# Channel mixer of a decoder block: partial products summed in PSUM banks, three token operands stored already split, gates applied to results

## The chip, the cores and the metric

The kernel runs on one core of a Trainium2 chip, as one program. The metric is the time of the whole program on the device, in microseconds (us); lower is better. A profile of one execution shows what each engine did: TensorE (PE, with PEld for its weight loads), VectorE (DVE), ScalarE (ACT), GpSimd (POOL) and SyncE (SP), whose queue issues most of the DMAs.

## The reference

The block takes 1024 tokens of 1024 features. It normalizes them, mixes tokens in two head groups, adds the result to the scaled input and normalizes again. The change lies in what follows, the channel mixer and the last norm:

```python
x = layer_norm(ALPHA * x + gt1 * mix, ln1_g, ln1_b)
h = x * (1.0 + sc2) + sh2
gu = h @ w_ffn_in                                     # 1024 x 1024 by 1024 x 5632
f = (silu(gu[..., :2816]) * gu[..., 2816:]) @ w_ffn_out   # 1024 x 2816 by 2816 x 1024
x = layer_norm(ALPHA * x + gt2 * f, ln2_g, ln2_b)
```

All of it is float32. The gates `gt1` and `gt2` are vectors over the 1024 output features.

## The kernel before

**Precision.** A float32 operand of a matmul is held as two parts: `hi`, the operand rounded (an ACT copy to the rounded type), and `lo`, the rest (a DVE subtraction). A product is three matmuls, hi x hi, hi x lo and lo x hi. Making the two parts is called a split here: one ACT and one DVE instruction on 128 x 512 elements, in `comb` (L1241 to L1247) for the first product and in `split2` (L1458 to L1463) for the second.

**Seven products for eight.** Each of the two large products is cut in halves of tokens, rows and columns and done in Winograd's form of Strassen's scheme, so that seven products of halves take the place of eight. The price is sums: of operands ahead of the products and of results behind them.

**First product** (`Col`, L1254 to L1313, and the loop at L1431). The 2816 hidden columns are 22 tiles of 128. For each the kernel loads 512 KB of gate weights and 512 KB of value weights. Seven times `prod` splits a 128 x 512 weight operand and runs 12 matmuls into one PSUM bank. Products `p1` and `p2` use the first half of the tokens (`a1h`, `a1l`), the other five (p5, p6, p7, p3, p4) use five sums of token halves (`a2h`, `a2l`: S3, S4, A22, S1, S2, made between L1413 and L1427). Each product has a PSUM bank of its own. The seven results are summed by DVE out of PSUM into SBUF tiles (`s1`, `u4`, `c22`; L1286, L1293, L1310). The sums of weights (`tsum`, L1396) are on POOL, and so are the two products with the silu (L1307, L1312). Two column tiles, kk and kk + 11, make a pair: from their results `f0`, `f1` POOL forms the sums (L1430, L1451) that become the seven token operands of the second product, QA11 to QS4, and SP's queue stores these in DRAM (`put`, L1442). The first three tiles' `p1` and `p2` are done earlier, among the transposes of the last token tiles.

**Second product** (`product`, L1504 to L1555). Seven calls, in the order QA11, QS1, QS2, QA22, QS3, QA12, QS4. Each goes through 11 steps of 128 rows. In a step the token operand `fs` and the weight operand `ws` are split into a ring of six tiles, and 12 matmuls run: three for each of four token tiles, each of which has a PSUM bank. `fs` comes from DRAM, two steps in one load. The weights are four blocks of 11 x 128 x 512: B11, B12, B21, B22. B11 is rewritten in place between the calls (T1 = B12 - B11, T2 = B22 - T1, T4 = T2 - B21) by DVE, B12 once by POOL (L1623, L1636, L1637, L1665), a step at a time in the functions `pre5`, `pre6`, `pre4`. Two operands, B21 and B22, take the gate `gt2` in their columns on POOL (L1666, L1695). The functions `done2` to `done7` (and `copied`) make generators that take results out of PSUM; `product` runs them a stage at a time between the steps of the next product (`pending`). They add gated results to the rows `R[t]`, which hold eight token tiles. `skip2` (L1493) has put the scaled and shifted first norm there, on POOL and DVE, during the second product. Each call takes four fresh banks. In the last call (`tail=5`) the matmuls of the last five steps are ordered by token tile, so that the banks finish one after the other. `norm2` (L1563) is the last norm of a token tile. In it POOL raises the variance to the power -1/2, ACT scales, POOL (and DVE for one half of tiles 0 to 2) applies gain and bias, and SP's queue stores. Tiles 4 to 7 get it during QA12, tiles 0 to 3 after QS4.

The order of instructions on each engine is decided when the program is compiled: the framework orders them by program order and its estimate of readiness, and inserts all semaphores. Instructions that go through `add` (L1560) keep their program order on their engine. On the chip each engine runs its list in order.

Of the kernel before, what the change touches and what calls it, by code (L numbers as in the profile page):

```python
# [9 lines left out]
F32 = mybir.dt.float32  # L10
# [61 lines left out]
SD0 = 8  # L72
GELU_A = math.sqrt(2.0 / math.pi)
# [4 lines left out]
def kernel(ctx, tc, inp, out, dbg=None):  # L78
# [12 lines left out]
    # ------------------------------------------------------------------ pools  # L91
# [26 lines left out]
    # -------------------------------------------------------------- constants  # L118
# [21 lines left out]
    # ------------------------------------- small vectors, one per partition  # L140
# [21 lines left out]
    for i, (n, ap) in enumerate(vecs):  # L162
# [9 lines left out]
        # the 32 gate columns stand three times side by side  # L172
# [13 lines left out]
    # derived columns: 1-mu (15), 0.5*w0, 0.5*a0, -, 0.5*k_a, 1-0.5*k_a, 0.5*sgg  # L186
# [7 lines left out]
    # --------------------------------------------------------- layer norm bits  # L194
# [11 lines left out]
    # ---------------------------------------------------------------- weights  # L206
# [40 lines left out]
    def ada(b, pool):  # L247
        """Half b of the columns of shift and scale: modc = silu(c) @ w_ada + b_ada."""
# [24 lines left out]
    with sctx:  # L273
# [8 lines left out]
        def hrs(hf):  # L282
            """Half hf of the tokens, normalized and feature-major."""
# [17 lines left out]
        for k in range(NK):  # L301
# [3 lines left out]
            # the small vectors come between the large ones  # L305
# [70 lines left out]
        with masks:  # L376
            # -------------------------------------------------------------- masks
# [43 lines left out]
            # chunk parity e keeps its removal-key scores, scaled by TS, on partitions 64 e  # L421
# [15 lines left out]
        # ------------------------------------- low-rank inputs of the decay, rate and gate  # L437
# [26 lines left out]
        # hi and lo parts; the 32 last rows carry hi, lo, hi against hi, hi, lo  # L464
# [23 lines left out]
        # ------------------------------------- spatial weights, transposed and masked  # L488
# [10 lines left out]
        # cgd[d, g, t] = 0.5 * (b[d] * sum_s W[t, s] + b_s[t])  # L499
# [14 lines left out]
    # ============================================ RWKV-7 and gMLP, feature-major  # L514
# [3 lines left out]
    # block diagonal over the two chunks of a tile  # L518
# [20 lines left out]
    def rwkv(q, hf, zr, zk, zv, carry):  # L539
# [37 lines left out]
        # ---- in-context rate (2a - 1)  # L577
# [6 lines left out]
        # ---- normalised removal key  # L584
# [17 lines left out]
        # ---- key, bonus  # L602
# [29 lines left out]
        # ---- scores: partition = (key, source token), free = (tile, parity, head, [A|R] target token)  # L632
# [36 lines left out]
        # ---- Z = (I - T)^-1 by doubling the size of the inverted diagonal blocks; Y = Z^T  # L669
# [24 lines left out]
        # T is held as 1024 T = T1 + T2 in halves of its width; the level masks carry 1 / 1024.  # L694
# [41 lines left out]
        # two correction terms bring the half-width inverse to full width:  # L736
        # E = I - Z (I - T), inverse = Z + E Z + E E Z
# [32 lines left out]
        # ---- U0 and A, solved  # L770
# [22 lines left out]
        # ---- chunk transition, its input, and the read-out rows  # L793
# [3 lines left out]
        # (tile, parity) = chunk; a parity has its own bank  # L797
# [32 lines left out]
        # ---- states  # L830
# [20 lines left out]
        # ---- read-out  # L851
# [10 lines left out]
        # ---- group norm, bonus, gate  # L862
# [24 lines left out]
    # ------------------------------------------------------------------ gMLP  # L887
# [16 lines left out]
    def late(c0, tail, side=iter(())):  # L904
        """The projections of four column tiles; the tail of each runs some steps into the next."""
# [66 lines left out]
    def modrest():  # L972
        # products and sums over the blocks of rows on the vector engine, the last sum on the tensor engine
# [58 lines left out]
    def mixout(t, wide=None):  # L1032
        """Token tile t of the output projection: two PSUM banks. The last rows of y come last."""
# [51 lines left out]
    def skip(t, x, ag, ab, second):  # L1085
        """alpha times the entry norm of token tile t."""
# [7 lines left out]
    def norm1(pool, t, x, sk, mo):  # L1094
        """x = the first norm of the skip and the output projection, without gain and bias."""
# [645 lines left out]
```

## Time and profile before

| | |
|---|---|
| Median of 3 runs | 1504.8 us (1504.12 to 1509.2) |
| Span of the profiled execution, first to last instruction | 1497.9 us |
| PE busy | 1356.2 us (91%) |
| DVE busy | 1062.1 us (71%) |
| POOL busy | 693.4 us (46%) |
| ACT busy | 509.2 us (34%) |
| Mean granted TensorE clock | 0.969 |
| First product's last part, second product's first matmul | up to 1206 us, 1206.3 us |
| Second product's last matmul ends | 1485.5 us |

The profiled execution's own time on the device was not recorded beside its span; the median of the runs lies 6.9 us above the span. Start times in the profile count from the start of the span. "Busy" is the time in which an engine had an instruction running, and matmuls overlap, so a busy PE may still run below its peak. In a group's row the first number after the bar is its busy time in us, then the mean in ns of one, and after the second bar the idle time ahead of it and what ended that. In a row of a stretch the columns are busy time and (count) for PE, PEld, DVE, ACT and POOL, then the granted TensorE clock as a share of full, the share of DMA engines' time in use, and GB/s. In a row of waits the columns are the total in us, how many, and the longest.

### The profile page before, as it was taken

How to read it: one execution, taken by the hardware profiler on the slowest of the kernel's cores; microseconds unless marked ns; L12 is line 12 of the kernel's file. 1: busy time of each engine (PE TensorE's matmuls, PEld its weight loads, DVE VectorE, ACT ScalarE, POOL GpSimd, SP SyncE). 2: the span in 40 equal slices, each digit the busy share in tenths (PEclk: the TensorE clock that was granted, in tenths of full speed). 3: DMA queues.
4: the chain of work that ended last, by engine and by line, in shares of the span. 5: the costliest groups of instructions: out<-in, count | busy, mean ns of one | idle time of the engine just before them, and what ended most of it. 6: DMA issues, size and time to landing. Idle time of an engine off the chain costs nothing. (4 is left out here: it accounts for less than half of the span.)

```text
span 1497.9 us, 23562 instructions
## 1 busy us (share of the span) xinstructions
PE 1356.2 (91%) x9279; PEld 1036.2 (69%) x9279; DVE 1062.1 (71%) x1615; ACT 509.2 (34%) x836; POOL 693.4 (46%) x596
## 2 busy tenths in 40 slices
PE   4879999999999998899879999999999997787986
PEld 3657666766766666667657888888888885565764
DVE  7734878786876887873899755555545458989997
ACT  4432323233232323331574333333333233332442
POOL 3672222121223244451457855555565327366584
PEclk9989999999999999999989999999999998898998
DMA  9423113222221222623403433323332278321222
GB/s 300 125 77 110 56 38 107 71 65 69 83 84 51 93 89 97 221 91 105 157 29 99 132 100 106 102 91 103 106 106 91 107 264 339 112 78 50 85 86 98
DMA packets 154057, 163.68 MB, mean 109 GB/s; under 512 B 9696, under 2 KB 111738, under 8 KB 153946
## 3 DMA queue, kind: packets, MB, share of 16 engines
q1 hardware_dynamic: 148810, 152.70, 31.4%
q10 hardware_dynamic: 4128, 6.32, 1.3%
q0 software_dynamic: 1008, 3.15, 0.6%
q8 instruction: 73, 1.20, 0.3%
q14 instruction: 38, 0.31, 0.1%
HBM read 124.65 MB, written 37.49 MB: 108 GB/s over the span
## 5 line engine op out<-in xcount | busy, mean ns | idle before, releaser
L1269 PE MATMUL p<-a2h,wc 128*128 128x512 f32 x440 | 173.7, 395 | 2.3 <-ACT wc L1245 2.3
L1271 PE MATMUL p<-a2h,wc 128*128 128x512 f32 x440 | 175.7, 400 | 0.0
L1270 PE MATMUL p<-a2l,wc 128*128 128x512 f32 x440 | 174.1, 396 | 0.0
L1513 PE MATMUL fo<-ws,fs 128*128 128x512 f32 x288 | 121.6, 422 | 39.7 <-DVE ws L1462 39.6
L229 PE MATMUL mm<-hh,wh 128*128 128x512 f32 x320 | 141.2, 441 | 2.8 <-ACT wh L216 2.8
L231 PE MATMUL mm<-hh,wl 128*128 128x512 f32 x320 | 132.0, 414 | 0.0
L230 PE MATMUL mm<-hl,wh 128*128 128x512 f32 x320 | 130.3, 407 | 0.0
L1512 PE MATMUL fo<-ws,fs 128*128 128x512 f32 x288 | 118.0, 413 | 4.6 <-ACT ws L1461 4.6
L1514 PE MATMUL fo<-ws,fs 128*128 128x512 f32 x288 | 118.6, 412 | 0.0
L1246 DVE TENSOR_TENSOR wc<-wr,wc 128x512 fp32r<-128x512 f32 x66 | 60.7, 921 | 74.9 <-ACT wc L1245 74.6
L1245 ACT ACTIVATE wc<-ts 128x512 fp32r<-128x512 f32 x88 | 55.1, 631 | 153.0 <-PE p L1271 136.5
L1513 PEld LDWEIGHTS fo<-ws,fs 128*128 128x128 f32 x288 | 57.5, 200 | 63.9 <-DVE ws L1462 52.5
L1269 PEld LDWEIGHTS p<-a2h,wc 128*128 128x128 f32 x440 | 82.9, 188 | 22.9 <-ACT wc L1245 3.3
L1270 PEld LDWEIGHTS p<-a2l,wc 128*128 128x128 f32 x440 | 83.0, 189 | 21.4 <-DVE a2l L1420 0.3
L1462 DVE TENSOR_TENSOR fs<-fr,fs 128x512 fp32r<-128x512 f32 x77 | 79.0, 1028 | 24.7 <-ACT fs L1461 24.6
L1271 PEld LDWEIGHTS p<-a2h,wc 128*128 128x128 f32 x440 | 82.9, 188 | 19.6 <-DVE wc L1246 0.3
L1462 DVE TENSOR_TENSOR ws<-b,ws 128x512 fp32r<-128x512 f32 x70 | 82.5, 1178 | 1.9 <-ACT ws L1461 1.6
L1398 POOL TENSOR_TENSOR ts<-ts,wr 128x512 f32<-128x512 f32 x22 | 30.3, 1377 | 106.1 <-DVE wc L1246 106.1
L1246 DVE TENSOR_TENSOR wc<-ts,wc 128x512 fp32r<-128x512 f32 x88 | 75.5, 862 | 2.9 <-ACT wc L1245 1.2
L1461 ACT ACTIVATE fs<-fr 128x512 fp32r<-128x512 f32 x77 | 47.9, 625 | 87.0 <-PE fo L1514 56.4
L229 PEld LDWEIGHTS mm<-hh,wh 128*128 128x128 f32 x320 | 60.9, 190 | 22.9 <-issue 6.7
L1269 PE MATMUL p<-a1h,wc 128*128 128x512 f32 x176 | 69.9, 397 | 3.9 <-ACT wc L1245 3.9
(518 smaller groups left out, 3379.5 us busy)
## 6 DMA issues: line engine op xcount, KB each, us to landing
wa<-in_w_ada_dram SPq DMA_DIRECT2D x48, 512.0 KB, 4.4
wr<-in_w_ffn_in_dram SPq DMA_DIRECT2D x44, 512.0 KB, 3.9
fr<-q SPq DMA_DIRECT2D x30, 512.0 KB, 3.8
wr<-in_w_in_dram SPq DMA_DIRECT2D x22, 512.0 KB, 4.3
q<-u SPq DMA_DIRECT2D x44, 256.0 KB, 3.2
q<-c SPq DMA_DIRECT2D x33, 256.0 KB, 2.2
b<-in_w_ffn_out_dram SPq DMA_DIRECT2D x6, 1024.0 KB, 13.0
x<-in_x_dram SPq DMA_DIRECT2D x8, 512.0 KB
```

The costliest lines, as they stand in the source:

```text
L229: T.matmul(ps[0:m, :], wh[:, k, 0:m], xh[:, k, cs], start=(k == 0), stop=False)
L230: T.matmul(ps[0:m, :], wh[:, k, 0:m], xl[:, k, cs], start=False, stop=False)
L231: T.matmul(ps[0:m, :], wl[:, k, 0:m], xh[:, k, cs], start=False, stop=(k == NK - 1))
L1245: A.activation(v[0], src, AF.Copy)
L1246: V.tensor_tensor(out=v[1], in0=src, in1=f(v[0]), op=ALU.subtract)
L1269: T.matmul(ps, w[:, 0, ks], h[:, o + k, :], start=k == 0, stop=False)
L1270: T.matmul(ps, w[:, 0, ks], l[:, o + k, :], start=False, stop=False)
L1271: T.matmul(ps, w[:, 1, ks], h[:, o + k, :], start=False, stop=k == 3)
L1462: V.tensor_tensor(out=t[:, 1, :], in0=src, in1=f(t[:, 0, :]), op=ALU.subtract)
L1512: T.matmul(pss[t], fs[:, 0, ts], ws[:, 0, :], start=kk == 0, stop=False)
L1513: T.matmul(pss[t], fs[:, 0, ts], ws[:, 1, :], start=False, stop=False)
L1514: T.matmul(pss[t], fs[:, 1, ts], ws[:, 0, :], start=False, stop=kk == NH - 1)
```

## The change

It edits the two products of the channel mixer and the last norm. Lines of comment that it also drops are not shown.

1. First product: the seven products of a column tile use three banks in place of seven. `p1` and the former `p2` share one, products of t2, t1 and u1 share `b`, two others share `e`. DVE reads a bank between the additions to it (two reads of `b` and one of `e` before the last one), and ACT reads `p1`'s. DVE has 5 sums per tile in place of 7. The weight sums t1 and t2 of the next tile are asked for in the middle of a tile (`ready`).
2. The sums of a pair's results move from POOL to DVE, and QA22, QS3 and QS4 are split there (`PAIRS`) and stored as hi and lo, 512 KB a step.
3. Scaled and shifted skip rows are made during the first product on DVE (`skip1`) and written back to DRAM; the second product only loads them.
4. Second product: the order is QA11, QS1, QA12, QS2, QS3, QS4, QA22. Two sets of four banks serve all seven; QA12, QS2, QS4 and QA22 add to what the bank holds. B12's difference moves to DVE; B21 becomes B21 - T2 in place of T4. The gate is applied to results by DVE (`gated`), not to columns of B21 and B22. The three stored pairs are loaded a step at a time and not split again.
5. Tiles 0 to 3 get their norm after QS4, tiles 4 to 7 after QA22, the last call.

```diff
+PAIRS = (4, 5, 6)
...
-        def rest(self):
-            s1 = self.s1
+        def sums(self):
             wu = self.load(FFN)
             self.u0, self.u1 = wu[:, 0:4, :], wu[:, 4:8, :]
+            t = w4.tile([P, 2, 4, P], F32, tag="w4", name="t12")
+            self.t1, self.t2 = t[:, 0, :, :], t[:, 1, :, :]
+            wdiff(self.t1, self.u0, self.g0)
+            wdiff(self.t2, self.u1, self.t1)
+        def rest(self, ahead):
+            s1 = self.s1
             add = lambda o, a, b: V.tensor_tensor(out=o, in0=a, in1=b, op=ALU.add)
-            t1 = tsum(self.u0, self.g0)
-            p5 = self.prod(pst("p5"), t1, a2h, a2l, OS1)
-            t2 = tsum(self.u1, t1)
-            p6 = self.prod(pst("p6"), t2, a2h, a2l, OS2)
-            add(s1, p6, s1)
+            b = self.prod(pst("pb"), self.t2, a2h, a2l, OS2)
+            u2 = tmp("u2")
+            add(u2, b, s1)
+            if self.sg is None:
+                self.prod(self.p1, self.g1, a1h, a1l, O2, True)
+                self.sg = tmp("sg")
+                A.activation(self.sg, self.p1, AF.Silu)
+            self.prod(b, self.t1, a2h, a2l, OS1, True)
             u4 = tmp("u4")
-            add(u4, p5, s1)
-            p7 = self.prod(pst("p7"), tsum(self.u1, self.u0), a2h, a2l, O3)
-            c22 = tmp("c22")
-            add(c22, p7, u4)
-            add(s1, p7, s1)
-            p3 = self.prod(pst("p3"), self.u1, a2h, a2l, O4)
-            add(u4, p3, u4)
-            G.tensor_tensor(out=u4, in0=u4, in1=self.sg, op=ALU.mult)
-            self.f0 = u4
-            p4 = self.prod(pmm("p4"), tsum(t2, self.g1), a2h, a2l, O22)
-            V.tensor_tensor(out=s1, in0=s1, in1=p4, op=ALU.subtract)
-            A.activation(s1, s1, AF.Silu)
-            G.tensor_tensor(out=c22, in0=c22, in1=s1, op=ALU.mult)
-            self.f1 = c22
+            add(u4, b, s1)
+            e = self.prod(pst("pe"), tsum(self.u1, self.u0), a2h, a2l, O3)
+            ahead()
+            add(u4, e, u4)
+            self.prod(b, self.u1, a2h, a2l, O4, True)
+            add(s1, b, s1)
+            G.tensor_tensor(out=s1, in0=s1, in1=self.sg, op=ALU.mult)
+            self.f0 = s1
+            self.prod(e, tsum(self.g1, self.t2), a2h, a2l, O22, True)
+            add(u2, e, u2)
+            A.activation(u2, u2, AF.Silu)
+            G.tensor_tensor(out=u4, in0=u4, in1=u2, op=ALU.mult)
+            self.f1 = u4
...
+    def skip1(t):
+        x = w4.tile([P, D], F32, tag="w4", name="xs")
+        rows = x1_dram[t * P:(t + 1) * P, :]
+        nc.sync.dma_start(x, rows)
+        V.tensor_tensor(out=x, in0=x, in1=rows1[0], op=ALU.mult)
+        V.tensor_tensor(out=x, in0=x, in1=rows1[1], op=ALU.add)
+        nc.sync.dma_start(rows, x)
-    sub = lambda o, a, b: G.tensor_tensor(out=o, in0=a, in1=b, op=ALU.subtract)
+    sub = lambda o, a, b: V.tensor_tensor(out=o, in0=a, in1=b, op=ALU.subtract)
...
+        c.rest(lambda: ready(i + 1))
+        if i == 3:
+            skip_rows()
+        if 4 <= i < 20 and i % 2 == 0:
+            skip1(i // 2 - 2)
...
+        def put(j, t):
+            if j in PAIRS:
+                t = f(split2(w4, "w4", t, "qp")).rearrange("p i n -> p (i n)")
+            nc.sync.dma_start(where(j), t)
...
-                    fs = split2(ring, "s", fr[:, kk - k0, :], "fs")
+                    if q in PAIRS:
+                        fs = wp.tile([P, 2, 512], F32R, tag="w", name="fp")
+                        dq.dma_start(f(fs).rearrange("p i n -> p (i n)"), q_dram[q][kk // 2][kk % 2])
+                    else:
...
+        def gated(t, n, src, out=None):
+            out = temp() if out is None else out
+            add(V, out, src, gt2[:, half(n)], ALU.mult)
+            yield
+            add(V, R[t][:, half(n)], R[t][:, half(n)], out)
...
-        product(QS2, B11, pa, pre=pre6, done=done6)
-        product(QA22, B11, pb, pre=pre4, done=done4)
-        product(QS3, B12, pa, pre=lambda k: add(G, B22[:, k, :], B22[:, k, :], gt2[:, half(1)], ALU.mult), done=done7)
-        product(QA12, B21, pb, done=done2)
-        product(QS4, B22, pa, tail=5, done=done3)
+        product(QA12, B21, psa, True, pre=pre2, done=done2)
+        product(QS2, B11, psb, True, pre=pre6, done=done6)
+        product(QS3, B12, psa, pre=pre7, done=done7)
+        product(QS4, B22, psb, True, done=done3, every=1)
+        product(QA22, B21, psa, True, tail=5, done=done4)
```

More of the change, by code (lines that the diff above doesn't have):

```diff
@@ L1252 @@
     order = [kk + NH * i for kk in range(NH) for i in range(2)]
+    QA11, QA12, QS1, QS2, QA22, QS3, QS4 = range(7)
     class Col:
@@ L1491, with product @@
         st2 = op.tile([P, 8, 2, 6], F32, tag="st2", name="st2")
[L1493 to L1500 removed]
         pending = []
[L1504 to L1507 removed]
+        def product(q, w, pss, more=False, pre=None, tail=0, done=None, every=2, ahead=(), dq=nc.sync):
             last = []
@@ L1541, in product @@
             for at, g in pending:
[L1542 removed]
+                if at == 0 or tail:
                     drain(g)
[L1544 removed]
+            pending[:] = [(0, g) for at, g in pending if at and not tail]
             g = None
@@ L1617, in pre1 @@
                 wfo(B12, 0, 1, 4 * (k - 8), min(4 * (k - 7), NH))
-        product(QA11, B11, pa, pre=pre1, ahead=ahead, dq=nc.scalar, done=copied(s1))
-        s5 = stile("s5")
-        def pre5(k):
-            add(V, B11[:, k, :], B12[:, k, :], B11[:, k, :], ALU.subtract)
-            if k == 2:
-                rows((gab[:, 0, :], inp["ln1_g"][0]), (gab[:, 1, :], inp["ln1_b"][0]))
-            if k % 3 == 1 and k < 8:
-                wfo(B22, 1, 1, (k - 1) // 3 * 4, min((k + 2) // 3 * 4, NH))
-            if k == 4:
-                A.activation(gab, gab, AF.Copy, scale=ALPHA)
-            if k > 4:
-                pending.append((0, skip2(k - 5)))
@@ L1633, with chunks, two @@
-        product(QS1, B11, pb, pre=pre5, done=copied(s5))
-        def pre6(k):
-            add(V, B11[:, k, :], B22[:, k, :], B11[:, k, :], ALU.subtract)
-            add(G, B12[:, k, :], B22[:, k, :], B12[:, k, :], ALU.subtract)
-            if k % 3 == 1 and k < 8:
-                wfo(B21, 1, 0, (k - 1) // 3 * 4, min((k + 2) // 3 * 4, NH))
+        def chunks(k, b, i, j):
+            if k % 3 == 1 and k < 8:
+                wfo(b, i, j, (k - 1) // 3 * 4, min((k + 2) // 3 * 4, NH))
+        def two(k, k0, o, a, b):
+            for x in range(2 * (k - k0), min(2 * (k - k0) + 2, NH)):
+                if x >= 0:
+                    diff(o, a, b, x)
@@ new lines, with pre2 @@
+        product(QA11, B11, psa, pre=pre1, ahead=ahead, dq=nc.scalar, done=copied(s1))
+        def pre5(k):
+            diff(B11, B12, B11, k)
+            chunks(k, B21, 1, 0)
+        product(QS1, B11, psb, pre=pre5, done=copied(s5))
+        def pre2(k):
+            if k in (0, 2, 4):
+                wfo(B22, 1, 1, 2 * k, min(2 * k + 4, NH))
+            if k in (1, 6):
+                for t in range(4):
+                    nc.sync.dma_start(R[t + 4 * (k // 6)], x1_dram[(t + 4 * (k // 6)) * P:(t + 4 * (k // 6) + 1) * P, :])
@@ L1686, in done7, with pre6, pre7 @@
+            add(V, x, u, x, ALU.subtract)
             yield
             yield
-            for n in range(2):
-                stats(t + 4, n)
+            yield from gated(t + 4, 0, x, x)
             yield
+        def pre6(k):
+            if k > 5:
+                diff(B12, B22, B12, k - 6)
+            if k == 6:
+                rows((lg, inp["ln2_g"][0]), (lb, inp["ln2_b"][0]))
+        product(QS2, B11, psb, True, pre=pre6, done=done6)
+        def pre7(k):
+            if k < 6:
+                diff(B12, B22, B12, k + 5)
+            two(k, 5, B21, B21, B11)
```

179 lines of the change are left out of this document (85 added, 94 removed).

## The prediction

> **What bounds the kernel now.** I read the page first, for the stages.
>
> ```profile
> span 1497.9 us, 23562 instructions
> ...
> PE 1356.2 (91%) x9279; PEld 1036.2 (69%) x9279; DVE 1062.1 (71%) x1615; ACT 509.2 (34%) x836; POOL 693.4 (46%) x596
> ...
> PE   4879999999999998899879999999999997787986
> ```
>
> PE is busy 91% of the span, so the holes matter more than the average. They lie in the last fifth, and that is where the edited code runs. The table by stretches then cuts this part up: the first product of the channel mixer (to 1206 us), and the second one in pieces chosen by how much POOL does.
>
> ```profile
> core 0: us, PE busy (x) PEld busy (x) DVE busy (x) ACT busy (x) POOL busy (x), PEclk, DMA share, GB/s
> 800.00:1206.00 406.00, 406.00 (x1750) 328.33 (x1749) 223.06 (x297) 124.90 (x204) 239.56 (x166) 1.00 0.33 107
> 1019.00:1058.20 39.20, 39.20 (x171) 31.71 (x170) 19.75 (x28) 12.36 (x20) 23.16 (x17) 1.00 0.33 103
> 1206.00:1486.00 280.00, 235.26 (x927) 181.88 (x925) 248.93 (x272) 101.09 (x172) 159.75 (x101) 0.93 0.39 137
> 1242.00:1300.00 58.00, 39.29 (x127) 27.96 (x126) 53.80 (x36) 15.79 (x26) 41.87 (x19) 0.82 0.59 218
> 1300.00:1316.00 16.00, 16.00 (x72) 13.26 (x71) 14.14 (x22) 7.85 (x13) 0.00 (x0) 1.00 0.43 144
> 1350.00:1400.00 50.00, 38.73 (x142) 29.08 (x140) 48.49 (x48) 14.87 (x26) 36.56 (x22) 0.90 0.18 59
> ```
>
> The first product is bound by PE: 406.00 of 406.00 us, granted clock 1.00, DVE at 55%. The second is not. Where POOL is idle (1300 to 1316) PE is full although DVE is busy for 14.14 of 16 us; where POOL works for three quarters of the time (1242 to 1300, 1350 to 1400) DVE is at 93 to 97%, PE falls to 39 of 58 and of 50, and the clock to 0.82 and 0.90. The view of waits names what PE stood for in the second product, and the timelines of DVE and POOL show why.
>
> ```profile
> PE fo L1513 <- DVE ws L1462: 39.6, 26, 3.6
> PE fo L1512 <- ACT ws L1461: 4.6, 4, 1.9
> 1234.01 0.68 DVE L1462 TENSOR_TENSOR ws<-b,ws 128x512 fp32r<-128x512 f32 x1
> 1234.61 0.69 DVE L1561 TENSOR_TENSOR b<-b,b 128x512 f32<-128x512 f32 x1
> 1245.41 16.23 POOL L1561 TENSOR_TENSOR r<-r,gab 128x1024 f32<-128x1024 f32 x6 [27.52 <-DMA fr<-q]
> 1253.79 2.86 DVE L1462 TENSOR_TENSOR fs<-fr,fs 128x512 fp32r<-128x512 f32 x1
> ```
>
> The same split takes 0.60 us from start to start when POOL rests, and 2.86 us beside POOL's skip rows (16.23 / 6 = 2.7 us each): the two take turns. So the second product is bound by DVE, and DVE by POOL.
>
> Its floor comes from PE's timeline: the second product's first matmul, one 82 matmuls later, and the last one.
>
> ```profile
> 1206.32 0.40 PE L1512 MATMUL fo<-ws,fs 128*128 128x512 f32 x1
> 1224.94 0.39 PE L1513 MATMUL fo<-ws,fs 128*128 128x512 f32 x1
> 1485.15 0.39 PE L1514 MATMUL fo<-wt,fs 128*128 128x512 f32 x1
> ```
>
> (1224.94 - 1206.32) / 82 = 0.227 us each; seven products of 11 steps x 4 banks x 3 are 924, so 210 us. They took 1485.5 - 1206.3 = 279.2. The excess is 69 us: 44 of waits (39.6 + 4.6), the other 25 in matmuls that ran slower under the lower clock.
>
> **The second product, part by part.** Removed from POOL are all its large jobs, in these rows:
>
> ```profile
> L1561 POOL TENSOR_TENSOR b<-b,gt 128x512 f32<-128x512 f32 x22 | 36.1, 1654 | 36.8 <-DVE b L1561 36.8
> L1561 POOL TENSOR_TENSOR r<-r,gab 128x1024 f32<-128x1024 f32 x8 | 21.9, 2751 | 27.5 <-DMA fr<-q 27.5
> L1561 POOL TENSOR_TENSOR b<-b,b 128x512 f32<-128x512 f32 x11 | 20.2, 1859 | 1.8 <-DVE b L1561 1.8
> L1462 DVE TENSOR_TENSOR ws<-b,ws 128x512 fp32r<-128x512 f32 x70 | 82.5, 1178 | 1.9 <-ACT ws L1461 1.6
> L1462 DVE TENSOR_TENSOR fs<-fr,fs 128x512 fp32r<-128x512 f32 x75 | 76.6, 1023 | 23.3 <-ACT fs L1461 23.2
> L1561 POOL TENSOR_TENSOR r<-r,lg 128x512 f32<-128x512 f32 x11 | 17.0, 1547 | 0.0
> ```
>
> The gates in two operands' columns (22), the skip (8) and the difference B12 (11) leave it, and so do the gates on partial results. What POOL keeps is the last norm: 14 gain and bias halves at about 1.5 us and 15 one-column jobs, some 30 us against 159.75, nearly all in the last of the seven products.
>
> DVE's list afterwards: 75 splits of ws; 42 of fs (four operands less the two made ahead; the three that come already split need none); 44 differences (B11 twice, B12, B21; 33 of them were there); and per token tile 3, 4, 4, 4 and 3 operations after the five products that end a sum, 72 for four tiles. That is 233, at 0.605 us 141 us, plus some 12 for the norms' halves and columns: 153 of 210 us, 73%. The densest product is QS3: 11 splits, 17 differences and 16 of the results' operations less one that slips out, 43 x 0.605 = 26 of 30 us, 87%. The row 1300 to 1316 has DVE at 88% and PE without a hole, so the row nearest to this load gives an excess of nothing. I keep 8 us of the 69 for the boundaries, where a product adds to banks that DVE or ACT has to have read, and for uneven bursts in QS3; the bounds are 2 and, if half the waits stay, 35. Worth -61.
>
> The loads: in the second product they were 42.6 MB (four B of 2.88, seven q of 2.88, x1 4.2, outputs 4.2, rows 2.5), and become 50 MB, since three operands double and two gain rows go. Over 218 us that is 230 GB/s, hidden behind PE as long as the 400 GB/s of the first row can be had (the last row is the stretch 1206 to 1300):
>
> ```profile
> 1236.00:1242.00 6.00, 6.00 (x28) 4.95 (x28) 5.16 (x8) 4.28 (x9) 0.00 (x0) 1.00 1.04 400
> fr<-q SPq DMA_DIRECT2D x30, 512.0 KB, 3.8
> b<-in_w_ffn_out_dram SPq DMA_DIRECT2D x6, 1024.0 KB, 13.0
> DMA packets 10728, 23.73 MB, mean 252 GB/s; under 512 B 656, under 2 KB 656, under 8 KB 10723
> ```
>
> SP's queue is passed by the moved x1 rows (eight of 512 KB, now in QA12 beside B22 and the gate row): 10.5 MB in 30 us, 350 GB/s, the tightest place. But by its end 24 MB are wanted, and 84 us at 400 make 33, so earlier issues cover it; an fs pair has five slots, 13.6 us, against 3.8 to 13.0 us of landing.
>
> **The first product.** Its matmuls stay 22 x 84. Per pair of columns (39.2 us, the row 1019 to 1058) DVE loses 4 sums and gains 4 subtractions or sums that were POOL's, 3 splits and, in eight pairs, two 128x1024 operations of the skip; the rows:
>
> ```profile
> L1293 DVE TENSOR_TENSOR s<-p,s 128x512 f32<-128x512 f32 x28 | 19.2, 686 | 18.0 <-PE p L1271 18.0
> L1246 DVE TENSOR_TENSOR wc<-wr,wc 128x512 fp32r<-128x512 f32 x42 | 33.5, 798 | 62.4 <-ACT wc L1245 62.2
> L1561 DVE TENSOR_TENSOR r<-r,gab 128x1024 f32<-128x1024 f32 x8 | 12.8, 1624 | 0.0
> L1430 POOL TENSOR_TENSOR u<-u,c 128x512 f32<-128x512 f32 x14 | 20.4, 1457 | 1.1
> ```
>
> 19.75 - 4 x 0.69 + 7 x 0.80 + 2 x 1.62 = 25.8 us of 39.2, 66%. POOL loses four jobs of 1.46 (23.2 to 17.3); ACT gains three splits (12.4 to 14.3). Stores and skip add 1.8 MB per pair to 4.0. All of this lies beside PE and costs nothing as throughput; were PE's cover gone, it would be 6 us per pair.
>
> What can cost is a wait that did not exist: matmuls now add to a bank that DVE or ACT reads midway. There are four such reads per column (s1, u2, u4, and u4 with the second bank), 85 in all because three columns have their gate already. Behind the waiting matmul stands everything on PE. Between the write and the next write stands one other product. How long that is, and how late DVE reads, is in these rows:
>
> ```profile
> 959.79 0.40 PE L1269 MATMUL p<-a2h,wc 128*128 128x512 f32 x1
> 972.16 0.40 PE L1271 MATMUL p<-a2h,wc 128*128 128x512 f32 x1
> 964.20 0.69 DVE L1293 TENSOR_TENSOR s<-p,s 128x512 f32<-128x512 f32 x1 [1.45 <-PE p L1271]
> 791.88 0.50 PE L1269 MATMUL p<-a2h,wc 128*128 128x512 f32 x1 [2.29 <-ACT wc L1245]
> 794.77 0.63 PE L1269 MATMUL p<-a2h,wc 128*128 128x512 f32 x1
> ```
>
> 53 matmuls in 12.37 us make 2.80 us for a product; DVE, which had waited 1.45 us for this product, reads it at once, and 0.69 later the bank is free: 2.1 us to spare, some three operations in front. For three columns the reader stands between two products on the same bank, 0.8 us each unless the order puts the second bank first, and the first product on the a2 operands now wants their last part (OS2) first. I take +6 us, 2 of them at the start; bounds 0 (PE was full, so no gain beyond the 2.29 at 791.88) and 20 (0.2 us at each read).
>
> The Trainium skill (TensorE: Matmul & The Clock Gate, "What's actually happening") has the clock halved only after an idle window of about 3.4 us, so stalls of a microsecond would cost themselves alone. The trace has matmuls of 0.63 us right after a gap of 2.29 us, so it can come sooner; by the rule the 14 us of stalls that I keep stay 14, and if each of 2 us brought ten slow matmuls they would be near 20.
>
> **The end.** The chain of waits ends in the last norm:
>
> ```profile
> 1485.94 0.68 DVE L1561 TENSOR_TENSOR r<-fo,r 128x512 f32<-128x512 f32 x1
> ...
> 1493.81 0.69 DVE L1561 TENSOR_TENSOR r<-r,lb 128x512 f32<-128x512 f32 x1
> ```
>
> From the last matmul (1485.5) to the end are 12.4 us. The gate on the result adds one DVE operation, 0.6. Worse, tiles 0 to 3 now get their norm inside the last product, where tiles 4 to 7 had theirs a product earlier: eight POOL halves of 1.5 us in front of the last four tiles' POOL jobs, and eight DVE halves in front of their first gate. DVE reaches them some 16 us into the last product, POOL is through 12 us later, and PE is done after 30; then the four last tiles queue at 3 to 4 us each. I take +5, bounds -1 and +13.
>
> **Sum.** 1497.9 - 61 + 6 + 5 = 1447.9 of span. The median of the runs, 1504.8, is 6.9 above the profiled execution's span; with that, 1455.
>
> **Rivals.** (a) DVE stays the bound in the second product: if the 205 operations on SBUF still took the 1.02 to 1.18 us of today's rows, they would be 225 us and with results and norms 250, 40 above the floor: about 1487. For it: QS3's 87%, bursts of five or six operations per 2.7 us step. Against it: POOL, the only partner in these turns, falls to 30 us. (b) The other side: the reads midway stop PE. If at each of the 85 DVE comes late because a subtraction that waits for POOL stands ahead in its queue, a stall of 0.66 us eats the 56 us that the other parts bring (56 / 85), and from there on the kernel is slower; at 1.0 it is 1504.8 - 56 + 85 = 1534. For it: DVE goes from half to two thirds busy. Against it: DVE waits for PE today, not PE for DVE, and 2.1 us are to spare.
>
> Here the Trainium skill speaks against the change: by PSUM — Partial Sum Buffer, "PSUM bank collisions raise a hardware error", two engines must be kept off one bank by semaphores, so none of these reads can overlap the next product on its bank. With no other product between, that would cost 0.75 at each; the rows show one between.
>
> (c) The doubled operands come late: at the 252 GB/s that loads averaged around 1250, 50 MB are 200 us, still under 218; only bunching at QA12 could cost, about 10 us: 1465. (d) The norms pile up at the end: 1463. That the work does not leave POOL at all is excluded by the diff.
>
> **Numbers.** My forecast with its own range (1438 to 1470, which takes in c and d) 0.75; (a), in part or whole, 1470 to 1495, 0.13; (b) 0.09, of which 0.05 is slower and the rest ends between 1480 and 1500; better than 1438 0.03. The range 1438 to 1480 leaves out under 2 in 10. About 0.3%, 4.5 us, is what a measurement tells from no change: faster 0.92, same 0.02, slower 0.06.
>
> **What would show it.** Second product: about 218 us from its first matmul to its last, granted clock near 1.00, DVE splits near 0.60 to 0.69 us, POOL near 30 us. First product: PE without holes over 1 us and its DVE share near 66%. End: 12 to 20 us after the last matmul. I am wrong if matmuls of the first product wait for DVE sums for tens of microseconds, if DVE is above 90% in the second product, or if PE there waits for operands loaded by DMA.

## The result and the profile after

The changed kernel takes 1658.8 us (median of 4 runs, 1654.98 to 1660.9) where the kernel before takes 1505.9 beside it: ratio 1.101, interval 1.0988 to 1.1037. The forecast was 1455 (range 1438 to 1480), so the sign is wrong. The profiled execution took 1654.98 us, its span is 1653.3.

The two traces cut at the same places, in us: from the first matmul on the a1 operands to the first of the second product (`fo`), from there to the end of the last matmul, and from there to the end.

| | start | first product | second product | end | span |
|---|---|---|---|---|---|
| before | 758.4 | 447.9 | 279.2 | 12.4 | 1497.9 |
| after | 757.8 | 652.5 | 227.2 | 15.8 | 1653.3 |
| difference | -0.6 | +204.6 | -52.0 | +3.4 | +155.4 |

The second product gained about what was forecast, the end lost about what was forecast, and the first product, which was to lose 6 us, lost 205. The page's head, two stretches of the table by windows (one answer for each), and PE's view of waits from 790 us on:

```profile
span 1653.3 us, 23399 instructions
...
PE 1385.5 (84%) x9279; PEld 1055.6 (64%) x9279; DVE 1025.2 (62%) x1661; ACT 499.1 (30%) x837; POOL 497.7 (30%) x479
...
PE   4979999999999898987767777686777768799995
```

```profile
805.00:1410.00 605.00, 453.74 (x1750) 352.80 (x1749) 274.03 (x343) 134.27 (x239) 175.06 (x122) 0.86 0.29 99
1426.00:1636.00 210.00, 205.82 (x895) 169.28 (x896) 153.44 (x255) 79.85 (x136) 19.08 (x22) 0.99 0.59 203
```

```profile
PE p L1275 <- ACT wc L1248: 136.5, 19, 8.9
PE pb L1275 <- ACT wc L1248: 17.6, 3, 8.9
PE fo L1551 <- ACT ws L1449: 10.2, 1, 10.2
PE fo L1551 <- DMA fp<-q: 4.0, 2, 2.3
PE pb L1276 <- DVE a2l L1438: 0.9, 1, 0.9
PE pe L1275 <- ACT wc L1248: 0.2, 1, 0.2
```

The columns of the windows are PE, PEld, DVE, ACT, POOL, granted clock, DMA share, GB/s. The same 1750 matmuls that took 406 us before take 605: PE is idle for 151 us, and at a clock of 0.86 the matmuls fill 454 us, 48 more than before. No engine has become the bound: DVE is at 45%, ACT at 22. PE waits for ACT's weight splits (`wc`, line 1248) at the start of every column but the first, 5.8 or 8.9 us each time. The view has no row for DVE's reads of a bank (`u`, line 1306): in this kernel PE waits for none of them. In the second product, from 1426 us on, PE is busy for 205.8 of 210 us, DVE at 73%, POOL for 19 us.

What PE waits for is seen where a column ends, in the timeline of the other engines:

```profile
946.74 0.69 DVE L1306 TENSOR_TENSOR u<-pe,u 128x512 f32<-128x512 f32 x1 [2.11 <-PE pe L1277]
947.46 0.63 ACT L1326 ACTIVATE u<-u 128x512 f32<-128x512 f32 x1 [11.34 <-DVE u L1306]
948.17 1.26 POOL L1327 TENSOR_TENSOR u<-u,u 128x512 f32<-128x512 f32 x1 [2.10 <-ACT u L1326]
...
949.46 0.63 ACT L1449 ACTIVATE qp<-u 128x512 fp32r<-128x512 f32 x1 [1.37 <-POOL u L1327]
949.46 1.74 DVE L1508 TENSOR_TENSOR u<-u,u 128x512 f32<-128x512 f32 x1 [2.03 <-POOL u L1327]
951.12 1.74 DVE L1450 TENSOR_TENSOR qp<-u,qp 128x512 fp32r<-128x512 f32 x1
...
953.62 0.69 DVE L1470 TENSOR_TENSOR s<-s,u 128x512 f32<-128x512 f32 x1
954.35 0.63 ACT L1449 ACTIVATE qp<-s 128x512 fp32r<-128x512 f32 x1 [4.26 <-DVE s L1470]
954.89 0.61 ACT L1248 ACTIVATE wc<-wr 128x512 fp32r<-128x512 f32 x1
955.40 0.61 ACT L1248 ACTIVATE wc<-t 128x512 fp32r<-128x512 f32 x1
955.55 0.80 PE L1275 MATMUL p<-a1h,wc 128*128 128x512 f32 x1 [8.85 <-ACT wc L1248]
```

In ACT's queue stand the silu of this column's last result, then the split of a stored pair (`qp`, line 1449), then that of a second pair, and only then the next column's first weight split. Each waits for a result of the column that PE has just ended (11.34, 1.37 and 4.26 us). The weight split needs none of them: its weights have long been loaded, and it runs at once when ACT gets there. Odd columns store two pairs (8.85 us), even ones one (5.78).

Before the change ACT ran ahead of PE through the same splits, and the end of a column made no difference:

```profile
989.35 0.63 ACT L1245 ACTIVATE wc<-ts 128x512 fp32r<-128x512 f32 x1 [2.17 <-PE p L1271]
992.15 0.63 ACT L1245 ACTIVATE wc<-ts 128x512 fp32r<-128x512 f32 x1 [2.17 <-PE p L1271]
992.81 0.64 ACT L1311 ACTIVATE s<-s 128x512 f32<-128x512 f32 x1
```

There a split waits for PE to free a slot, one per product of 2.8 us, and the silu finds its result ready.

### The profile page after: what moved, and what is told of

Same layout as the page of the kernel before. It is cut to its first block, busy times and chain, and to the rows that moved or that the text cites. A ratio compares the mean times of both kernels' runs of the same rounds, so it can differ in the third digit from the quotient of the medians.

```text
span 1653.3 us, 23399 instructions
## 1 busy us (share of the span) xinstructions
PE 1385.5 (84%) x9279; PEld 1055.6 (64%) x9279; DVE 1025.2 (62%) x1661; ACT 499.1 (30%) x837; POOL 497.7 (30%) x479
## 4 chain that ended last, share of the span: by engine, by line
PE 60%; DVE 15%; POOL 9%; issue 7%; DMA 4%; ACT 3%; SPq 0%; ACTq 0%; POOLq 0%; DVEq 0%
PE mm L230 4%; PE pb L1277 4%; PE pb L1275 4%; PE pb L1276 4%; PE fo L1551 4%; PE fo L1553 4%; PE fo L1554 4%; PE mm L232 3%; PE mm L231 3%; PE p L1275 3%; PE p L1277 3%; PE p L1276 3%; POOL u L1327 2%; DVE s L1470 2%; POOL s L1322 1%
## 5 line engine op out<-in xcount | busy, mean ns | idle before, releaser
L1275 PE MATMUL p<-a1h,wc 128*128 128x512 f32 x176 | 88.3, 502 | 140.4 <-ACT wc L1248 140.0
L1275 PEld LDWEIGHTS p<-a1h,wc 128*128 128x128 f32 x176 | 43.3, 246 | 157.5 <-ACT wc L1248 148.7
L1275 PE MATMUL pb<-a2h,wc 128*128 128x512 f32 x264 | 107.3, 406 | 17.7 <-ACT wc L1248 17.6
L1276 PE MATMUL pb<-a2l,wc 128*128 128x512 f32 x264 | 106.6, 404 | 0.9 <-DVE a2l L1438 0.9
L1277 PE MATMUL pb<-a2h,wc 128*128 128x512 f32 x264 | 107.3, 406 | 0.0
L1277 PE MATMUL p<-a1h,wc 128*128 128x512 f32 x176 | 83.9, 477 | 2.4 <-DVE wc L1249 2.4
L1276 PE MATMUL p<-a1l,wc 128*128 128x512 f32 x176 | 84.4, 480 | 0.0
L1551 PE MATMUL fo<-ws,fs 128*128 128x512 f32 x176 | 69.5, 395 | 10.2 <-ACT ws L1449 10.2
L1275 PEld LDWEIGHTS pb<-a2h,wc 128*128 128x128 f32 x264 | 51.3, 194 | 31.9 <-ACT wc L1248 18.9
L232 PEld LDWEIGHTS mm<-hh,wl 128*128 128x128 f32 x320 | 61.2, 191 | 14.9 <-issue 1.5
L1277 PE MATMUL pe<-a2h,wc 128*128 128x512 f32 x176 | 70.2, 399 | 0.0
L1275 PE MATMUL pe<-a2h,wc 128*128 128x512 f32 x176 | 69.8, 396 | 0.2 <-ACT wc L1248 0.2
L1276 PE MATMUL pe<-a2l,wc 128*128 128x512 f32 x176 | 69.9, 397 | 0.0
```

The source lines that it names most:

```text
L232: T.matmul(ps[0:m, :], wl[:, k, 0:m], xh[:, k, cs], start=False, stop=(k == NK - 1))
L1275: T.matmul(ps, w[:, 0, ks], h[:, o + k, :], start=k == 0 and not more, stop=False, skip_group_check=more)
L1276: T.matmul(ps, w[:, 0, ks], l[:, o + k, :], start=False, stop=False, skip_group_check=more)
L1277: T.matmul(ps, w[:, 1, ks], h[:, o + k, :], start=False, stop=k == 3, skip_group_check=more)
L1551: T.matmul(pss[t], fs[:, 0, ts], ws[:, 0, :], start=kk == 0 and not more, stop=False, skip_group_check=more)
```

## The theories

**1** (mine): the pair splits draw from the same 12 slots (`w4`) as the weight splits. Slots are given out in the order of the program, and the lists of the engines that fill them follow. So the next column's weight splits come behind the pairs, and the pairs behind the column's last results. **2**: the sums kept in PSUM stop PE, by the reads midway or otherwise (the forecast's rival b). **3**: ACT's work, or the silu alone, holds the splits up. **4**: 12 slots are too few, now that differences, skip rows and pairs live in them.

## Experiments on the loss

**Stored once.** The three operands go out unsplit and are split in the second product like the others.

```
-PAIRS = (4, 5, 6)
+PAIRS = ()
```

> After the change, but the three operands (QA22, QS3, QS4) are stored once, unsplit, and split by ACT and DVE in the second product like the others (PAIRS = ()). Theory 1 (the split at the store takes its turn among the weight splits on ACT and so holds back the next column's splits until the column's last results are there): no hole of more than 2 us per column in the first product, its 200 us come back, the 33 further splits are hidden in the second product (DVE there from 74% to about 86%): 1450 to 1470. Theory 2 (the sums kept in PSUM and the reads midway stop PE): 1620 or more. Theory 4 (too few of the 12 slots for weights, differences and skip rows): holes stay in part, 1540 to 1620.

1462.3 us (before: 1504.1; ratio 0.9713, 0.9688 to 0.9738). Theory 1's figure: nearly 200 us come back, though the sums stay in PSUM and are read midway. Theory 2 falls as the cause of the loss. PE's waits in the first product, from 790 us on, the worst of them now for DVE's read of a bank (`u`, line 1306):

```profile
PE pb L1275 <- DVE u L1306: 6.3, 4, 3.5
PE pb L1275 <- ACT wc L1248: 2.9, 1, 2.9
PE pb L1276 <- DVE a2l L1438: 0.9, 1, 0.9
PE pe L1275 <- ACT wc L1248: 0.5, 1, 0.5
```

**Pairs in two slots of their own.** The split pairs are kept; the weights, differences and rows get 10 slots.

```
-    w4 = fi.enter_context(tc.tile_pool(name="w4", bufs=12))
+    w4 = fi.enter_context(tc.tile_pool(name="w4", bufs=10))
+    qpp = fi.enter_context(tc.tile_pool(name="qpp", bufs=2))
...
-                t = f(split2(w4, "w4", t, "qp")).rearrange("p i n -> p (i n)")
+                t = f(split2(qpp, "qp", t, "qp")).rearrange("p i n -> p (i n)")
```

> After the change, but the stored pairs have two slots of their own, and the weight splits, differences and skip rows 10 instead of 12; as much work as after, on the same engines. Theory 1: the splits at the store no longer stand in the weights' order; 1450 to 1465. Theory 2: 1620 or more. Theory 4 (too few slots): with 10 it gets no better, 1650 or more. Theory 3 (the load on ACT and the silu in front of the splits by themselves): 1600 or more, since ACT has the same work.

1459.8 us (ratio 0.9712, 0.9689 to 0.9735). The same work on the same engines, fewer slots for the weights, and the loss is gone: theories 3 and 4 fall too. ACT's list at the end of a column now reads

```profile
943.59 0.63 ACT L1249 ACTIVATE wc<-wr 128x512 fp32r<-128x512 f32 x1 [3.46 <-PE pb L1278]
946.39 0.63 ACT L1249 ACTIVATE wc<-ts 128x512 fp32r<-128x512 f32 x1 [2.17 <-PE pe L1278]
947.11 0.64 ACT L1327 ACTIVATE u<-u 128x512 f32<-128x512 f32 x1
950.40 0.63 ACT L1450 ACTIVATE qp<-u 128x512 fp32r<-128x512 f32 x1 [2.65 <-POOL u L1328]
950.94 0.58 ACT L1286 ACTIVATE s<-p 128x512 f32<-128x512 f32 x1
```

ACT still waits 2.65 us for POOL's result, but the weight splits stand in front. The last row reads the bank of the next column's first product: PE has done that product while ACT waited.

**The same slots, the pairs later in the program.** A column's stores, with their sums and splits, are held until five weight splits of the next column have been written: they become functions (`odd`, and `even` for the other columns) that `flush` calls.

```
-        c.rest(lambda: ready(i + 1))
+        c.rest(lambda: (ready(i + 1), flush()))
...
-        else:
+        def odd(c=c, lo=lo if i % 2 else None, put=put):
             put(QA12, c.f0)
...
+            held.append(odd)
```

> After the change with the same slots, engines and work; only the place in the program of the stores of a column (their sums, pair splits and DMAs) is moved: they come after five weight splits of the next column instead of before them. Theory (slots are given out in the program's order, and the lists of ACT and DVE follow it): the holes of 5.8 and 8.9 us go, 1455 to 1475. If the mere sharing of 12 slots, or the pairs' work on ACT and DVE, held PE up: 1600 or more.

1472.6 us (ratio 0.9788, 0.9763 to 0.9812), as expected. Slots, engines and work are those of after; the place in the program alone is worth 186 us. What is left over the run with own slots is mostly one wait of 10.1 us at the start of the second product, where the last pairs still stand in front of its first splits. It is the row `fo ... <- ACT ws` of after's waits, and own slots remove it.

**The high part of a pair by DVE.** ACT no longer touches the pairs, which take their turn in the 12 slots as in after.

```
-                t = f(split2(w4, "w4", t, "qp")).rearrange("p i n -> p (i n)")
+                s = w4.tile([P, 2, 512], F32R, tag="w4", name="qp")
+                V.tensor_copy(s[:, 0, :], t)
+                V.tensor_tensor(out=s[:, 1, :], in0=t, in1=f(s[:, 0, :]), op=ALU.subtract)
+                t = f(s).rearrange("p i n -> p (i n)")
```

> After the change, but the high part of each stored pair is written by DVE instead of ACT; the pairs still take their turn in the same 12 slots as the weight splits, so that the next column's splits still stand in ACT's list behind the silu of the column before, but no longer behind the pair's split. Theory 1 in the form 'ACT's in-order list: silu, pair split, and only then the burst of weight splits': the hole per column shrinks from 5.8 and 8.9 us to what the silu's chain alone takes, 1 to 3 us, and little clock is lost: 1480 to 1540. If the turn in the slots itself holds the splits back (a slot is given out only once the pair before it is written, whoever writes it): 1640 or more. If the pair's split on ACT was all of it: 1455 to 1470.

1671.9 us (two runs; ratio 1.1127, 1.1084 to 1.117). My figure for ACT's list alone (1480 to 1540) was wrong. The time is the one expected if the turn in the slots itself held the splits back, but the timeline shows another reason:

```profile
954.59 0.63 ACT L1326 ACTIVATE u<-u 128x512 f32<-128x512 f32 x1 [11.34 <-DVE u L1306]
955.12 0.61 ACT L1248 ACTIVATE wc<-wr 128x512 fp32r<-128x512 f32 x1
...
956.61 1.47 DVE L1498 CAST qp<-u 128x512 fp32r<-128x512 f32 x1 [2.05 <-POOL u L1327]
...
962.30 0.69 DVE L1499 TENSOR_TENSOR qp<-s,qp 128x512 fp32r<-128x512 f32 x1
962.91 0.68 DVE L1249 TENSOR_TENSOR wc<-wr,wc 128x512 fp32r<-128x512 f32 x1
...
963.65 0.80 PE L1277 MATMUL p<-a1h,wc 128*128 128x512 f32 x1 [7.13 <-DVE wc L1249]
```

ACT's splits follow the silu at once, and PE's hole there shrinks to 1.96 us in every column. But the low parts of the same splits are DVE's, and in DVE's list they stand behind the pairs: the wait moves to the third matmul, 7.13 us here and 4.12 in the next column. The slot itself is no obstacle when the kernel runs (ACT writes `wc` at 955.12, before the pair, whose turn came first, is written from 956.61 on). It is the order of the lists, on each engine that writes into these slots. This kernel locates the wait; the two before it show that the order is the cause.

## Experiments on the parts

**The second part alone.** The first product's columns as before the change (seven banks, sums on DVE), stored unsplit; the second product of after, and the skip rows scaled during the first product.

```
-        def sums(self):
-        def rest(self, ahead):
+        def rest(self):
...
-PAIRS = (4, 5, 6)
+PAIRS = ()
```

> The second part alone: the first product as before the change (seven banks, sums on DVE as before, no splits at the store) with the second product of after (sums in PSUM, gates on results, skip rows scaled during the first product). All theories that place the loss in the first product's new code: 1450 to 1462, 45 to 55 faster than before, with PE full in both products. If the second product's gain needed the stored pairs, 1465 to 1485 (DVE with 33 more splits at over 90%).

1446.7 us (ratio 0.9616, 0.9599 to 0.9634), 3 us below the expected 1450 to 1462. First product 447.9 us, as before; second 211.2, one above the floor of 210; end 26.3.

**The first part alone.** Sums in two banks, stored unsplit, no skip rows; the second product of before.

```
-        if i == 3:
-            skip_rows()
-        if 4 <= i < 20 and i % 2 == 0:
-            skip1(i // 2 - 2)
...
-        product(QA11, B11, psa, pre=pre1, ahead=ahead, dq=nc.scalar, done=copied(s1))
+        product(QA11, B11, pa, pre=pre1, ahead=ahead, dq=nc.scalar, done=copied(s1))
...
```

> The first part alone, without the splits at the store and without the skip rows: sums kept in two PSUM banks in the first product, then the second product as it was before the change. Theory 1: 1500 to 1512, as before, since the reads midway stand beside another product. Theory 2: 1620 or more. Rival b of the forecast in its own size (0.66 to 1 us at each of 85 reads): 1560 to 1590.

1524.8 us (ratio 1.0141, 1.0119 to 1.0163), 21 slower: more than theory 1's 1500 to 1512, less than rival b's 1560 to 1590. First product 471.5 us, 23.6 more than before. PE waits for DVE's reads at 11 of the 85 places:

```profile
PE pb L1275 <- DVE u L1306: 13.3, 11, 3.5
```

The run stored once shows such a place, in its timeline of PE and DVE:

```profile
807.36 1.78 DVE L1249 TENSOR_TENSOR wc<-ts,wc 128x512 fp32r<-128x512 f32 x1
...
808.15 0.40 PE L1277 MATMUL pb<-a2h,wc 128*128 128x512 f32 x1
809.06 2.35 DVE L1249 TENSOR_TENSOR wc<-t,wc 128x512 fp32r<-128x512 f32 x2
...
811.33 0.68 DVE L1306 TENSOR_TENSOR u<-pb,s 128x512 f32<-128x512 f32 x1
...
812.06 0.60 PE L1275 MATMUL pb<-a2h,wc 128*128 128x512 f32 x1 [3.52 <-DVE u L1306]
```

The product ends at about 808.5, and DVE reads it at 811.33: the rest of one weight split and two more, slow beside POOL, stand in front of the read. That is rival b's lateness, with slow splits in place of a subtraction that waits for POOL, and at 3 to 12 places a run (12 with the pairs later) instead of 85.

**Alternating banks.** As stored once, in the order b, e, b, e, b, so that another product always stands between two on a bank. The products of a column in their new order:

```
             b = self.prod(pst("pb"), self.t2, a2h, a2l, OS2)
+            e = self.prod(pst("pe"), tsum(self.u1, self.u0), a2h, a2l, O3)
             self.prod(b, self.t1, a2h, a2l, OS1, True)
+            self.prod(e, tsum(self.g1, self.t2), a2h, a2l, O22, True)
             self.prod(b, self.u1, a2h, a2l, O4, True)
```

> As the run with the operands stored once, but the products of a column alternate between the two banks (b, e, b, e, b), so that between two products on a bank always stands another one, in the first three columns too. Theory: of the 16 us that this first product costs more than the one before the change, 8 to 11 are DVE reads that come late in the first columns, where nothing stood between; 1448 to 1456. If those reads are not the cause (the lost time is the start, waiting for the last part of the a2 operands): 1460 to 1465.

1460.6 us (ratio 0.9716, 0.9690 to 0.9742), no difference from stored once that can be told. The time is the alternative's, but its reason isn't confirmed: the waits for DVE's reads stay (5.5 us at three places, after 6.3 at four). One product between (2.8 us) doesn't cover a read that stands behind splits. How the remaining 13 us divide between these reads, the start on the a2 operands and the clock stays open.

## Experiments on the end

Without pairs the second product is on its floor, and the end doubles to 26 us. In the last product DVE is late with the norms:

```profile
1412.37 1.66 DVE L1587 TENSOR_TENSOR r<-r,lb 128x512 f32<-128x512 f32 x1
1413.95 1.78 DVE L1587 TENSOR_TENSOR r<-r,lg 128x512 f32<-128x512 f32 x1
...
1419.16 1.65 DVE L1587 TENSOR_TENSOR r<-r,lb 128x512 f32<-128x512 f32 x1
1420.73 0.68 DVE L1587 TENSOR_TENSOR v<-fo,gt 128x512 f32<-128x512 f32 x1
```

These are rows of the second part alone: seven of DVE's eight halves (gain or bias on half a row) take 1.7 us beside POOL's eight, and the first result of the last product is read at 1420.73, after PE's last matmul (1419.7).

**The norm on DVE alone** (no half on POOL).

```
-                    e = V if n and t < 7 else G
+                    e = V
```

> As the second part alone, but gain and bias of the last norm are all put on by DVE; POOL had one half of each row. Theory: beside POOL an operation of DVE takes 1.7 us instead of 0.69, so that the half that POOL takes over costs DVE more than it saves: DVE reaches the last four tiles 3 us earlier (16 x 0.65 = 10.4 instead of 13.5 us for tiles 0 to 3) and the end after the last matmul shrinks from 26.5 to 19 to 23: 1438 to 1443. If DVE's count of operations decides, 3 to 8 us slower: 1449 to 1455.

1443.5 us (ratio 0.9607, 0.9588 to 0.9626), half a microsecond above the expected range. The interval overlaps that of the second part alone, so the trace has to tell: the end is 23.2 instead of 26.3 us, and DVE does twice as many halves in less time, the first result read 2.6 us earlier:

```profile
1416.82 0.68 DVE L1587 TENSOR_TENSOR r<-r,lg 128x512 f32<-128x512 f32 x1
1417.54 0.69 DVE L1587 TENSOR_TENSOR r<-r,lb 128x512 f32<-128x512 f32 x1
1418.15 0.68 DVE L1587 TENSOR_TENSOR v<-fo,gt 128x512 f32<-128x512 f32 x1
```

The Trainium skill (SBUF — State Buffer, "Who interferes with whom") says that an instruction of DVE with two inputs in SBUF contends with one of GpSimd that reads SBUF. The rows agree: 0.69 us alone, 1.65 to 1.78 beside POOL.

**Pairs in their own slots, on the second part alone.**

```
-PAIRS = ()
+PAIRS = (4, 5, 6)
...
+                t = f(split2(qpp, "qp", t, "qp")).rearrange("p i n -> p (i n)")
```

> As the second part alone, with the three operands stored as split pairs again, these in two slots of their own. Theory: 33 splits leave DVE's and ACT's last three products, the norms of tiles 0 to 3 are done when the last product ends, and the end after the last matmul is near the 16 us of after instead of 26.5; the first product stays full: 1434 to 1442. Rival: the pairs' loads (0.5 MB each step) stand behind the result stores on SP's queue and stop PE by as much as the end gains: 1443 to 1449.

1440.1 us (ratio 0.9590, 0.9567 to 0.9613), as expected. The end is 15.8 us, the second product 214.5: 3.0 us of that are waits for the pairs' loads, the rival's mechanism at a third of the gain.

**Both: pairs in their own slots and the norm on DVE.**

```
-                    e = V if n and t < 7 else G
+                    e = V
```

> The second part alone with the pairs in two slots of their own, and the last norm's gain and bias all on DVE. Theory: DVE's chain over the last four tiles shrinks from 25 to about 21.5 us, as no operation takes 1.7 us beside POOL; the first product and the loads are as in the run with the pairs' own slots: 1435 to 1438. If the two gains are the same one (DVE late at the last tiles, which the pairs have mended already): 1439 to 1442.

1435.8 us (ratio 0.9556, 0.9527 to 0.9586), in the expected range, but not by the expected way. The end is only 0.6 us shorter (15.2 us), so there the two gains are mostly the same one. The second product is 2.9 us shorter (211.7), with 1.4 us of waits for the pairs' loads in place of 3.0; why these came earlier stays open. The interval overlaps that of the run before.

**The last product's pairs on ACT's queue,** on top of both.

```
-        product(QA22, B21, psa, True, tail=5, done=done4)
+        product(QA22, B21, psa, True, tail=5, done=done4, dq=nc.scalar)
```

> As the run before in this list, and the pairs of the last product are loaded through ACT's queue instead of SP's, where they stand behind result stores. Theory: the 3.0 us that PE waits for them go: 1432 to 1436. If ACT, waiting to issue a load until a slot is free, holds back the weight splits behind it: 1438 to 1446.

1436.3 us (ratio 0.9547, 0.9528 to 0.9565), just above the expected 1432 to 1436. The other queue brings nothing that can be told: of the 3.0 us that it was to save, PE's wait for the pairs was down to 1.4 already, and it is 1.3 with it. Both of these last kernels beat the one before the change, by 4.4 and 4.5%, and the changed one, by 13%.

## Why the prediction was wrong

- **First product, +6 (bounds 0 and 20): wrong, and the step is known.** It listed what ACT and DVE gain and said "All of this lies beside PE and costs nothing as throughput; were PE's cover gone, it would be 6 us per pair". As throughput that holds (DVE 45%, ACT 22%). But the three added splits per pair of columns draw on the weights' slots, and nobody asked what stands behind them on ACT and DVE. The holes, 8.85 + 5.78 = 14.6 us per pair of columns, are the 151 us of idle time, and the half clock after them the 48 us of slower matmuls; the remaining 6 of the +205 fall before 805 us. The forecast looked for what stands behind a waiting instruction only at PE's new waits ("Behind the waiting matmul stands everything on PE"), not at the waits that the stores brought to ACT.
- **The reads midway: right in kind, mis-sized.** Of the +6, 2 were for the start. In the changed kernel itself PE waits for none of the reads. Where the holes are gone, the first product is longer than before by 13.0 us (alternating banks), 15.0 (stored once), 16.4 (own slots), 21.8 (pairs later) and 23.6 (first part alone), the last two above the bound. "2.1 us to spare" forgot that DVE's own list can hold the read back longer.
- **Rival b: its mechanism is real, its extent isn't.** It needed 0.66 us at each of 85 reads; none was late in the changed kernel, and 3 to 12 in the runs without the holes, by 0.3 to 3.5 us. The kernel did become slower, by another wait than b's. No rival had it.
- **Second product, -61: right.** -52.0 in after and -68.0 without pairs, PE full at a clock of 0.99 behind the first 16 us, DVE at 73% as forecast, POOL 22 us, and 30 up to the end of the program, as forecast. The 8 us kept for boundaries were not needed; the 10.2 us hole at its start is the first product's fault again, and 4 us are waits for the pairs' loads. Rivals (a) and, but for those 4 us, (c) fall.
- **End, +5: right for after (+3.4),** because the pairs take 33 splits from DVE; without them it is +13.9, just above the bound of 13 (rival (d)'s pile-up), and the reason given (DVE and POOL late with the norms) is the one seen.
- On the Trainium skill's two rules: no run shows a collision in PSUM, and the reads cost what DVE's lateness makes them. On the clock, see below; the side sum "near 20" is too low, since ten matmuls at 0.43 us from start to start (after, from 956.15 us on) in place of 0.23 cost 2 us per stall, 14 us in seven stalls, which makes 28. The forecast's own sum doesn't use it.

## What to carry to other kernels

A new tile in an existing pool joins that pool's order: what it waits for, everything allocated after it may wait for, on every engine that writes the pool. So when an operation with a late input is added, list what stands behind it on its engine and what shares its slots, even where the engine is a fifth busy. Give late work its own slots, or put it later in the program, behind the early work of the next step.

## What the runs showed of the hardware

The granted clock changes in steps of 3.41 us. In each of the thirteen traces of this case every stretch at half clock lasts a whole number of such steps, one to seven, and all of them start whole numbers of steps apart. Cut along these steps, the run stored once, around its hole of 1.80 us at 839.21, gives (the columns are PE, granted clock, DMA share, GB/s):

```profile
836.21:839.63 3.42, 1.62 (x8) 1.00 0.89 279
839.63:843.04 3.41, 3.41 (x10) 0.50 0.30 114
843.04:846.45 3.41, 3.41 (x17) 1.00 0.68 225
```

The hole lies within one step, which leaves PE 1.62 us of work in it, and the next step is at half clock: a matmul takes 0.63 us there in place of 0.39. The run with the pairs later has a longer hole, of 2.94 us, at 1163.01:

```profile
1158.19:1161.60 3.41, 1.88 (x9) 1.00 0.13 39
1161.60:1165.02 3.42, 2.01 (x9) 1.00 0.84 290
1165.02:1168.43 3.41, 3.41 (x16) 1.00 0.02 5
```

Two steps share it, and the clock stays. All thirteen traces, from 780 us on, say the same. Take the steps at full clock in which PE stood idle for some time: after all 158 with less than 1.65 us of idle time the clock stayed full, after all 79 with more than 1.95 us it was halved, and after the 12 between it was either. The line lies near half a step. As the ends of matmuls are modelled, it can't be drawn more sharply. Each hole of 5.8 or 8.9 us in the changed kernel crosses it, which cost 48 us over 21 holes, 2.3 us each.

The Trainium skill (TensorE: Matmul & The Clock Gate, "What's actually happening") has a free-running window of about 3.4 us, and the length of the stretches agrees. It also has the clock halved after an idle window; the hole of 1.80 us, with matmuls on both sides, shows that a window needn't be wholly idle. The counts above put the line near half a window. In the forecast the rule stood as "stalls of a microsecond would cost themselves alone", and for the holes of 0.93 us in the first part alone that holds: the clock stays at 1.00 from 900 to 1200 us.
